# Attention scores as three fp32r products instead of one fp32 product, with the order of layer 0's blocks made anew

## The chip, the cores and the metric

The kernel runs on one core of a Trainium2 chip. The metric is the device time of one execution in microseconds; the table below gives the median of three runs and the time of the one execution that was profiled.

## The reference, cut to what matters

A decoder of two layers over 256 tokens of width 1024, all in float32. The change touches the attention of layer 0 ("stick-breaking" attention, 16 heads of 64 columns). In its core:

```python
qkv = (h @ w_qkv).reshape(b, s, 3, SB_HEADS, HEAD_DIM)
q, k, v = qkv[:, :, 0], qkv[:, :, 1], qkv[:, :, 2]
...
z = jnp.einsum('bqhd,bshd->bhqs', q_blk, k).astype(jnp.float32) * scale
causal = key_pos[None, :] < t[:, None]
log_1m = jnp.where(causal, jax.nn.log_sigmoid(-z), 0.0)
excl = lax.cumsum(log_1m, axis=3, reverse=True) - log_1m
a = jnp.where(causal, jnp.exp(jax.nn.log_sigmoid(z) + excl), 0.0)
return jnp.einsum('bhqs,bshd->bqhd', a.astype(v.dtype), v)
```

After that come the output projection, a squared-ReLU MLP, the second layer (native sparse attention and another MLP) and a last norm. None of these is edited.

## The kernel before, in words

Tokens are two tiles of 128 (T = 2). Weights arrive in pieces of 1 MB on the queue of SyncE. Each is split into a high part of type float32r (`wh`, a copy by ScalarE at line 135) and a low part, the remainder (`wl`, a subtraction by VectorE at line 138), in two halves of 1024 columns. Large products then use float32r operands: high times high, high times low and low times high. The helper `wide` (line 199) does this for products with a split activation: one matmul of 512 columns takes the high weights against both parts of the activation, one of 256 columns takes the low weights against the high part. `W` (line 143) and `step` (line 150) bring the splits in, up to two weights ahead of the one in use.

Layer 0 works on pairs of heads, eight in all, each pair filling 128 partitions. For each pair, `proj` (line 487) forms the transposed queries and keys: for each of two halves (queries, then keys), 8 matmuls of 512 columns (`qk<-xa,wh`) and 8 of 256 (`qk<-xa,wl`), 32 in all. ScalarE copies the second part out of PSUM (line 504), VectorE adds the first (line 505), and the sum is scaled with the norm's factor (line 506), on GpSimd for queries and on VectorE for keys. The result, `qkT`, is float32.

Three kinds of block follow for each pair p:

- S, `scores(p)` (line 509): four float32 matmuls of the two heads, each head in its own half of the array's rows (64 of 128), into one PSUM bank per head: 256 columns for the second tile of tokens, 128 for the first. Then the softmax-like chain: minimum with a cap on VectorE (line 525), Exp and Ln on ScalarE (529, 530), a scan (531) and a subtraction (532) on VectorE, Exp on ScalarE (533). A small memset on GpSimd (522) comes first.
- T, `turn(p)` (line 536): six transposes on TensorE of the full array, evicted by ScalarE (line 545).
- V, `values(p)` (line 548): four float32 matmuls of 64 columns of the array each (half of it per head), evicted as high and low parts (271, 272).

What stands where is written out in the table `INS` (line 38). An entry (m, k, f, p) calls block f of pair p ahead of product k of projection m; m = 8 is the output projection, where k counts slots of six matmuls each. The program's order of instructions is only a wish: a scheduler puts an instruction that is not ready by its own reckoning behind others on its engine. `high_priority` moves an eviction ahead. Once the schedule is made, each engine runs its instructions in that order.

Of the kernel before, what the change touches and what calls it, by code (L numbers as in the profile page):

```python
# [7 lines left out]
F32 = mybir.dt.float32  # L8
F32R = mybir.dt.float32r
# [5 lines left out]
P = 128  # L15
D = 1024
T = 2
NK = D // P
NH = 16
DH = 64  # L20
# [15 lines left out]
ROW = 3 * SEG  # L36

INS = (
# [4 lines left out]
)  # L43

NSA = (
# [17 lines left out]
def hybrid_kernel(ctx, tc, x, xca, xcb, eye, gcols, gfin, wqk, wva, wvb, wo0, wkv, wq, wg, rot, wo1, w1, w2, cw1, cw2, cpos, gate_b, cmask, consts, out):  # L63
    nc = tc.nc
# [8 lines left out]
    def f32(a):  # L73
        return a.bitcast(F32)
# [8 lines left out]
    def bank(name, dt=F32):  # L83
        return ps.tile([P, 512], dt, tag="a", name=name, bufs=4)

    def bank2(name):
        return ps.tile([P, 512], F32, tag="z", name=name, bufs=4)
# [55 lines left out]
    def W(i, n=None, keep=None):  # L143

        while at[0] < i or at[0] == i and n is not None and at[1] < n or at[0] == i and n is None:
            split()
        cur[0] = max(cur[0], i if keep is None else keep)
        return made[i]

    def step(k=1, end=None, pin=False):  # L150
        for _ in range(k):
            if at[0] < min(cur[0] + 3, end or len(stream)):
                split(pin)
# [30 lines left out]
    def pe(ins):  # L184
        if strict[0]:
            tc.keep_in_program_order(ins)
# [6 lines left out]
    def mm(o, a, b, first, last):  # L193
        pe(nc.tensor.matmul(o, a, b, start=first, stop=last, skip_group_check=True))  # L194
# [4 lines left out]
    def wide(o, a, xt, k, part, first, last):  # L199


        if part == 0:
            mm(o, a[0], xt[2][:, k, :, :], first, False)
        else:
            mm(o[:, 0:T * P], a[1], xt[0][:, k, :], False, last)
# [7 lines left out]
    def cut(hl, a, b):  # L213
        return hl[0][:, a:b], hl[1][:, a:b]
# [178 lines left out]
    def layer0(ap):  # L393
# [93 lines left out]
        def proj(p, hooks={}):  # L487

            w = W(i_qk[p])
            qkT = ap.tile([P, 2, T * P], F32, name="qkT", bufs=3)  # L490
            for half in range(2):
                qk = bank("qk") if p else bank2("qk")
                for j in range(2 * NK):
                    if j == 0:
                        step()
                    for f in hooks.get(2 * NK * half + j, ()):
                        f()
                    i, k = divmod(j, NK)
                    o = half * D + k * P
                    wide(qk, cut(w, o, o + P), xt, k, i, k == 0, k == NK - 1)  # L500
                lo = ap.tile([P, T * P], F32, name="qlo", bufs=2)
                o = qkT[:, half, :]
                with tc.high_priority(offset=300):
                    nc.scalar.copy(lo, qk[:, T * P:2 * T * P])
                    nc.vector.tensor_add(o, qk[:, 0:T * P], lo)
                    (nc.vector if half else nc.gpsimd).tensor_tensor(o, o, rbq[:, half], op=OP.mult)
            live[p] = qkT

        def scores(p):


            qkT = live[p]
            qT, kT = qkT[:, 0, :], qkT[:, 1, :]
            z = [bank2(f"z{hd}") for hd in range(2)]
            for hd in range(2):
                r = slice(hd * DH, (hd + 1) * DH)
                mm(z[hd][:, 0:256], qT[r, P:2 * P], kT[r, :], True, False)
            for hd in range(2):
                r = slice(hd * DH, (hd + 1) * DH)
                mm(z[hd][:, 256:384], qT[r, 0:P], kT[r, 0:P], False, True)  # L520
            e = ap.tile([P, 2 * ROW], F32, name="sbe", bufs=3)
            nc.gpsimd.memset(e.rearrange("p (b c) -> p b c", b=6)[:, :, P:SEG], NEG)
            cap = cst[:, C_CAP:C_CAP + 3 * P].rearrange("p (b c) -> p b c", b=3)
            for hd in range(2):
                nc.vector.tensor_tensor(
                    e[:, hd * ROW:(hd + 1) * ROW].rearrange("p (b c) -> p b c", b=3)[:, :, 0:P],
                    z[hd][:, 0:384].rearrange("p (b c) -> p b c", b=3), cap, op=OP.min)
            s = ap.tile([P, 2 * ROW], F32, name="sbs", bufs=2)
            nc.scalar.activation(s, e, AF.Exp)
            nc.scalar.activation(s, s, AF.Ln, bias=1.0)  # L530
            nc.vector.tensor_tensor_scan(s[:, ::-1], s[:, ::-1], go_on[:, ::-1], 0.0, OP.add, OP.mult)
            nc.vector.tensor_sub(e, e, s)
            nc.scalar.activation(e, e, AF.Exp)
            live[p] = e
# [24 lines left out]


        do = {"S": scores, "T": turn, "V": values}

        def inside(n):
# [6 lines left out]
        for n in range(NP):  # L570
            proj(n, inside(n))
# [537 lines left out]
```

## Time and profile before

| | |
|---|---|
| median of 3 runs | 616.9 us (616.69 to 617.33) |
| profiled execution | 618.14 us, of which the span of instructions is 616.4 us |
| TensorE busy | 605.6 us, 98% of the span |
| VectorE busy | 423.2 us, 69% |
| ScalarE busy | 342.2 us, 56% |
| GpSimd busy | 60.0 us, 10% |
| layer 0's projections | 28.5 to 86.75 us of the span |

The profile shows one execution. PE stands for TensorE's matmuls, PEld for its weight loads, DVE for VectorE, ACT for ScalarE, POOL for GpSimd. A row of the timeline gives start, length, engine, line, operation, output and inputs, the part of the array in use (rows * columns), the operand's shape and how many instructions were merged. Ends of matmuls are modelled, so the length of a row on PE holds some time after the next one has begun; the distance between starts is the better measure. L194 is a helper that issues most matmuls, so blocks are told apart by the names of their tiles: `qk` for the projections, `z` for S, `pa` for T, `po` for V, `acc` for the output projection.

### The profile page before, as it was taken

The page shows a single profiled execution, that of the slowest core. Times are in us where ns is not written, and L with a number is a line of the kernel's source. Part 1 is how long each engine was busy: PE and PEld are TensorE (multiplying, and loading weights), DVE is VectorE, ACT ScalarE, POOL GpSimd, SP SyncE. Part 2 cuts the span into 40 slices and gives each one's busy share as a digit, 9 for nine tenths or more (in the row PEclk, how much of TensorE's full clock was granted, in tenths as well). Part 3 has the DMA queues.
Part 4 walks back from the last instruction along what each step waited for, and adds up shares of the span by engine and source line. Part 5 has one row for each costly group of instructions (what it writes and reads, how often), then busy time and mean ns, then how long its engine had stood idle before and what let it go on. Part 6 is the DMA issues. An engine that isn't in the chain of part 4 may idle for free.

```text
span 616.4 us, 8955 instructions
## 1 busy us (share of the span) xinstructions
PE 605.6 (98%) x3477; PEld 507.1 (82%) x3477; DVE 423.2 (69%) x692; ACT 342.2 (56%) x598; POOL 60.0 (10%) x81
## 2 busy tenths in 40 slices
PE   9999999999999999999999989999999999999996
PEld 5888887888888888888998678677888888888885
DVE  5598996876666665666697799755766666556655
ACT  6667765674454444543762598854654444444441
POOL 0201110000000000000330255440000000000000
PEclk9999999999999999999999999999999999999999
DMA  8963331645555455554387831311474545545501
GB/s 308 356 265 137 137 137 69 233 176 211 199 198 196 158 204 200 192 203 153 116 258 284 277 133 69 105 68 61 152 267 158 203 187 205 204 156 198 193 1 68
DMA packets 18810, 109.33 MB, mean 177 GB/s; under 512 B 2512, under 2 KB 3792, under 8 KB 6736
## 3 DMA queue, kind: packets, MB, share of 16 engines
q1 hardware_dynamic: 17472, 107.06, 47.8%
q10 hardware_dynamic: 1296, 1.70, 0.8%
q8 instruction: 27, 0.44, 0.3%
q14 instruction: 15, 0.12, 0.1%
HBM read 106.66 MB, written 1.05 MB: 175 GB/s over the span
## 4 chain that ended last, share of the span: by engine, by line
PE 90%; DVE 3%; DMA 3%; issue 2%; ACT 1%; SPq 0%; POOLq 0%; POOL 0%; DVEq 0%; ACTq 0%
PE pu L194 29%; PE acc L189 12%; PE acc L190 11%; PE acc L191 11%; PE qk L194 7%; PE po L194 3%; PE z L194 2%; PE pk L191 2%; PE pk L189 2%; PE pk L190 2%; DMA wc<-in_cw 2%; PE ptp L197 2%; PE pv L190 1%; PE pv L191 1%; PE pv L189 1%
## 5 line engine op out<-in xcount | busy, mean ns | idle before, releaser
L138 DVE TENSOR_TENSOR wl<-raw,wh 128x1024 fp32r<-128x1024 f32 (+1 forms) x192 | 226.0, 1209 | 120.2 <-ACT wh L135 113.5
L135 ACT CAST wh<-raw 128x1024 fp32r<-128x1024 f32 (+1 forms) x192 | 190.6, 1031 | 106.4 <-PE acc L191 40.9
L194 PE MATMUL pu<-xn,wh 128*128 128x512 f32 x512 | 132.2, 392 | 0.0
L194 PEld LDWEIGHTS pu<-xn,wh 128*128 128x128 f32 x512 | 93.7, 188 | 18.0
L189 PE MATMUL acc<-wh,hh 128*128 128x512 f32 (+1 forms) x256 | 100.2, 391 | 0.0
L190 PE MATMUL acc<-wl,hh 128*128 128x512 f32 (+1 forms) x256 | 99.9, 390 | 0.0
L191 PE MATMUL acc<-wh,hl 128*128 128x512 f32 (+1 forms) x256 | 99.1, 389 | 0.0
L194 PE MATMUL pu<-xn,wl 128*128 128x256 f32 x512 | 76.5, 282 | 0.0
L194 PEld LDWEIGHTS pu<-xn,wl 128*128 128x128 f32 x512 | 72.1, 190 | 5.1
L191 PEld LDWEIGHTS acc<-wh,hl 128*128 128x128 f32 x256 | 48.1, 188 | 10.7 <-DVE hl L368 0.8
L189 PEld LDWEIGHTS acc<-wh,hh 128*128 128x128 f32 x256 | 48.2, 188 | 10.1 <-ACT hh L367 1.2
L190 PEld LDWEIGHTS acc<-wl,hh 128*128 128x128 f32 x256 | 48.2, 188 | 8.7
L367 ACT CAST hh<-ms 128x512 fp32r<-128x512 f32 x32 | 19.8, 620 | 63.1 <-DVE ms L363 63.1
L359 ACT COPY mr<-pu 128x256 f32<-128x256 f32 x64 | 23.6, 369 | 27.2 <-PE pu L194 27.2
L368 DVE TENSOR_TENSOR hl<-ms,hh 128x512 fp32r<-128x512 f32 x32 | 22.1, 692 | 19.2 <-ACT hh L367 19.2
L194 PE MATMUL qk<-xa,wh 128*128 128x512 f32 x128 | 32.5, 394 | 0.0
L360 DVE TENSOR_TENSOR mu<-pu,mr 128x256 f32<-128x256 f32 x64 | 26.6, 418 | 7.0 <-ACT mr L359 7.0
L887 POOL TENSOR_TENSOR pe<-pe,rs 128x512 f32<-128x512 f32 (+1 forms) x32 | 28.3, 917 | 25.5 <-DVE rs L882 13.6
L873 ACT ACTIVATE pe<-pe,nm 128x256 f32<-128x256 f32 (+1 forms) x64 | 28.2, 443 | 4.3 <-DVE nm L871 3.0
L194 PEld LDWEIGHTS qk<-xa,wh 128*128 128x128 f32 x128 | 22.9, 188 | 4.3 <-issue 0.2
L189 PE MATMUL acc<-wh,oT 128*128 128x512 f32 x64 | 26.3, 411 | 0.0
L191 PE MATMUL acc<-wh,oT 128*128 128x512 f32 x64 | 25.1, 392 | 0.0
(195 smaller groups left out, 828.4 us busy)
## 6 DMA issues: line engine op xcount, KB each, us to landing
raw<-in_w SPq DMA_DIRECT2D x64, 1024.0 KB, 4.8
raw<-in_wqk SPq DMA_DIRECT2D x8, 1024.0 KB, 5.1
raw<-in_wo SPq DMA_DIRECT2D x8, 1024.0 KB, 4.8
raw<-in_wkv SPq DMA_DIRECT2D x6, 1024.0 KB, 4.9
raw<-in_wq SPq DMA_DIRECT2D x4, 1024.0 KB, 6.7
wc<-in_cw SPq DMA_DIRECT2D x4, 1024.0 KB, 9.9
raw<-in_wvb SPq DMA_DIRECT2D x5, 512.0 KB, 7.1
raw<-in_wva SPq DMA_DIRECT2D x6, 256.0 KB, 5.3
```

The lines of the kernel that those rows point to most:

```text
L135: ins = nc.scalar.copy(h[:, r], raws[j][:, r])
L138: nc.vector.tensor_sub(lo[:, r], raws[j][:, r], f32(h[:, r]))
L189: pe(nc.tensor.matmul(o, a[0], b[0], start=first, stop=False, skip_group_check=True))
L190: pe(nc.tensor.matmul(o, a[0], b[1], start=False, stop=False, skip_group_check=True))
L191: pe(nc.tensor.matmul(o, a[1], b[0], start=False, stop=last, skip_group_check=True))
L194: pe(nc.tensor.matmul(o, a, b, start=first, stop=last, skip_group_check=True))
L359: nc.scalar.copy(r[:, q], pu[:, 256:512])
L360: nc.vector.tensor_add(u[:, q], pu[:, 0:256], r[:, q])
L367: nc.scalar.copy(hh, sv)
L368: nc.vector.tensor_sub(hl, sv, f32(hh))
L873: nc.scalar.activation(e, e, AF.Exp, scale=-1.0, bias=nm[:, hd, t, b:b + 1], accum_out=rs[:, hd, t, b:b + 1])
L887: nc.gpsimd.tensor_tensor(sv, sv, rs[:, hd, t, :][:, :, None].to_broadcast([P, 2, n]), op=OP.mult)
```

## The change

The scaled queries and keys are kept as two float32r parts, a high one copied by ScalarE and a low one subtracted by GpSimd, for each of the 16 halves. The scores become three products: high times high, high times low, low times high, for each head and each tile of tokens: twelve matmuls for a pair, the two heads in turn. The table `INS` is written anew.

```diff
 INS = (
-    (1, 0, 'S', 0), (3, 8, 'T', 0), (3, 24, 'S', 1), (3, 24, 'S', 2), (3, 24, 'V', 0), (4, 28, 'T', 1),
-    (5, 12, 'T', 2), (5, 16, 'V', 1), (5, 24, 'S', 3), (5, 24, 'S', 4), (5, 24, 'V', 2), (6, 29, 'T', 3),
-    (7, 12, 'T', 4), (7, 24, 'V', 3), (7, 24, 'V', 4), (7, 24, 'S', 5), (7, 24, 'S', 6), (8, 3, 'S', 7),
-    (8, 5, 'T', 5), (8, 6, 'T', 6), (8, 8, 'V', 5), (8, 8, 'V', 6), (8, 10, 'T', 7), (8, 11, 'V', 7),
+    (1, 6, 'S', 0), (3, 16, 'T', 0), (3, 18, 'S', 1), (3, 22, 'V', 0), (3, 29, 'S', 2), (4, 23, 'T', 1),
+    (5, 3, 'V', 1), (5, 16, 'T', 2), (5, 17, 'S', 3), (5, 19, 'V', 2), (5, 25, 'S', 4), (6, 24, 'T', 3),
+    (7, 17, 'T', 4), (7, 21, 'S', 5), (8, 0, 'V', 3), (8, 0, 'V', 4), (8, 0, 'S', 6), (8, 6, 'S', 7), (8, 6, 'T', 5),
+    (8, 7, 'T', 6), (8, 8, 'V', 5), (8, 8, 'V', 6), (8, 9, 'T', 7), (8, 10, 'V', 7),
 )
...
-            qkT = ap.tile([P, 2, T * P], F32, name="qkT", bufs=3)
+            qkT = ap.tile([P, 2, 2, T * P], F32R, name="qkT", bufs=3)
...
                 lo = ap.tile([P, T * P], F32, name="qlo", bufs=2)
-                o = qkT[:, half, :]
+                o = ap.tile([P, T * P], F32, name="qsum", bufs=2)
+                h, l = qkT[:, half, 0], qkT[:, half, 1]
                 with tc.high_priority(offset=300):
                     nc.scalar.copy(lo, qk[:, T * P:2 * T * P])
                     nc.vector.tensor_add(o, qk[:, 0:T * P], lo)
                     (nc.vector if half else nc.gpsimd).tensor_tensor(o, o, rbq[:, half], op=OP.mult)
+                    nc.scalar.copy(h, o)
+                    nc.gpsimd.tensor_sub(l, o, f32(h))
...
-            qT, kT = qkT[:, 0, :], qkT[:, 1, :]
             z = [bank2(f"z{hd}") for hd in range(2)]
-            for hd in range(2):
-                r = slice(hd * DH, (hd + 1) * DH)
-                mm(z[hd][:, 0:256], qT[r, P:2 * P], kT[r, :], True, False)
-            for hd in range(2):
-                r = slice(hd * DH, (hd + 1) * DH)
-                mm(z[hd][:, 256:384], qT[r, 0:P], kT[r, 0:P], False, True)
+            for t in (1, 0):
+                o, n = (256, P) if t == 0 else (0, 2 * P)
+                for i, (a, b) in enumerate(((0, 0), (0, 1), (1, 0))):
+                    for hd in range(2):
+                        r = slice(hd * DH, (hd + 1) * DH)
+                        mm(z[hd][:, o:o + n], qkT[r, 0, a, t * P:(t + 1) * P], qkT[r, 1, b, 0:n],
+                           t == 1 and i == 0, t == 0 and i == 2)
```

## The prediction

> **What bounds the kernel now.** I read the page first: span, busy shares, clock and the chain of work that ended last.
>
> ```profile
> span 616.4 us, 8955 instructions
> PE 605.6 (98%) x3477; PEld 507.1 (82%) x3477; DVE 423.2 (69%) x692; ACT 342.2 (56%) x598; POOL 60.0 (10%) x81
> PEclk9999999999999999999999999999999999999999
> PE 90%; DVE 3%; DMA 3%; issue 2%; ACT 1%; SPq 0%; POOLq 0%; POOL 0%; DVEq 0%; ACTq 0%
> ```
>
> The span is PE's: 98% busy, at full clock throughout, and 90% of the last chain. The change lies in layer 0 from the first projection (28.5 us) to the output projection, so next I took the busy times of that stretch.
>
> ```profile
> 28.50:86.75 58.25, 58.25 (x385) 49.39 (x384) 51.80 (x71) 43.27 (x69) 8.55 (x13) 1.00 0.48 176
> 86.75:112.00 25.25, 25.09 (x137) 19.67 (x136) 18.82 (x23) 15.95 (x25) 0.00 (x0) 1.00 0.25 92
> ```
>
> After stretch and length stand PE, PEld, DVE, ACT and POOL. PE has no hole in the first stretch, DVE is 89% busy (51.80 of 58.25), ACT 74%, POOL 15%. So here a microsecond of PE time is a microsecond of span, and DVE is next in line. The timeline of PE then gives what each block costs. First S (scores) of pair 0, which stands alone among the projection's products:
>
> ```profile
> 34.18 2.00 PE L194 MATMUL qk<-xa,wh 128*128 128x512 f32 x8
> 36.02 1.12 PE L194 MATMUL qk<-xa,wl 128*128 128x256 f32 x8
> 36.97 0.86 PE L194 MATMUL qk<-xa,wh 128*128 128x512 f32 x3
> 37.76 0.92 PE L194 MATMUL z<-qkT 64*128 64x256 f32 x8
> 38.61 1.42 PE L194 MATMUL qk<-xa,wh 128*128 128x512 f32 x5
> 39.87 1.11 PE L194 MATMUL qk<-xa,wl 128*128 128x256 f32 x8
> ```
>
> Starts are what counts, since ends overlap. Eight wide products take 36.02 - 34.18 = 1.84 us (0.230 each), eight narrow ones 36.97 - 36.02 = 0.95 us (0.119 each). From 36.97 to 39.87 lie 2.90 us with eight wide products in them, so S alone costs 2.90 - 1.84 = 1.06 us. Now two S and one V (values) in one run, and two V and two S:
>
> ```profile
> 49.86 2.00 PE L194 MATMUL qk<-xa,wh 128*128 128x512 f32 x8
> 51.79 1.58 PE L194 MATMUL z<-qkT 64*128 64x256 f32 x16
> 53.30 0.87 PE L194 MATMUL po<-sbt,v 128*64 128x256 f32 x8
> 54.10 1.22 PE L194 MATMUL qk<-xa,wl 128*128 128x256 f32 x8
> 55.16 2.00 PE L194 MATMUL qk<-xa,wh 128*128 128x512 f32 x8
> ...
> 80.80 2.00 PE L194 MATMUL qk<-xa,wh 128*128 128x512 f32 x8
> 82.74 1.52 PE L194 MATMUL po<-sbt,v 128*64 128x256 f32 x16
> 84.19 1.58 PE L194 MATMUL z<-qkT 64*128 64x256 f32 x16
> 85.69 1.22 PE L194 MATMUL qk<-xa,wl 128*128 128x256 f32 x8
> 86.75 0.40 PE L189 MATMUL acc<-wh,oT 128*128 128x512 f32 x1
> ```
>
> The first S takes 38.61 - 37.76 = 0.85 to the next block, two take 53.30 - 51.79 = 1.51, so a further S is 0.66 us of pure work. One V takes 54.10 - 53.30 = 0.80, two 84.19 - 82.74 = 1.45: a further V is 0.65. S alone cost 1.06, so going into the half-array form and back costs 0.40, 0.20 for each change of form. Three changes in S S V: 55.16 - 49.86 = 5.30, less 1.84 and 0.95, is 2.51, of which 1.97 is work: 0.18 each. Three in V V S S: 5.95 - 2.79 = 3.16, of which 2.62 is work: 0.18. I take 0.19. A switch between forms is a visible price that joined blocks share. T (transposes) has no such price:
>
> ```profile
> 46.41 2.01 PE L194 MATMUL qk<-xa,wh 128*128 128x512 f32 x8
> 48.26 0.82 PE L543 MATMUL pa<-ident,sbe 128*128 128x128 f32 x6
> 48.83 1.19 PE L194 MATMUL qk<-xa,wl 128*128 128x256 f32 x8
> ```
>
> It starts 1.85 us after eight wide products began, without a gap, and delays the next by 1.03 - 0.95 = 0.08; 0.65 in all.
>
> The Trainium skill, TensorEngine Tiling (Array Packing), Key Properties, says that changing the tiling mode drains TensorE; the trace agrees, with 0.18 to 0.20 us a change, and by that rule it would hold for fp32r as well, against this change: the 1.5 us below stand with it and go without it.
>
> **The change, part by part.**
>
> *The products.* Before, a pair's scores are four fp32 products, recorded as eight matmuls, two each. After, they are twelve fp32r products: for each head three of 256 columns and three of 128. The two heads run beside each other in the two row halves: 16 records in 1.51 us before, though taken one by one at the paces of full fp32r products (0.119 for 256 columns, 0.111 for 128, below) they would need 8 x 0.119 + 8 x 0.111 = 1.84. So I count a head pair as one.
>
> ```profile
> 608.97 0.27 PE L190 MATMUL accq<-wl,hh 128*128 128x128 f32 x1
> ...
> 610.09 0.28 PE L191 MATMUL accq<-wh,hl 128*128 128x128 f32 x1
> ```
>
> These are fp32r products of 128 columns, ten steps in 1.12 us: 0.111 each, hardly under the 0.119 of 256 columns, because the weight load before each is as long for both. S becomes 3 x 0.119 + 3 x 0.111 = 0.69 us instead of 0.66: **+0.03 x 8 = +0.25 us**. The 256-column half gains, and the 128-column half, where the load sets the pace, loses it again. No trace shows fp32r in row halves. Bounds: if pace followed columns (0.119 and 0.06), S would be 0.54 and the eight a gain of 1.0 us; if heads took turns, 6 x 0.119 + 6 x 0.111 = 1.38 and a loss of 5.8 us. I take 0.69, from the nearest rows.
>
> *The places.* I count changes of form along both tables. Before: S0; S1 S2 V0; V1; S3 S4 V2; V3 V4 S5 S6; S7; V5 V6; V7, which is 2+3+2+3+3+2+2+2 = 19. After: S0 to S5 and V0 to V2 each stand alone (18), then V3 V4 S6 (3), S7, V5 V6 and V7 (2 each): 27. T is a full-array transpose and needs no change. **8 x 0.19 = +1.5 us.**
>
> *The one stall that goes.*
>
> ```profile
> 90.63 0.39 PE L191 MATMUL acc<-wh,oT 128*128 128x512 f32 x1
> 91.18 0.92 PE L194 MATMUL z<-qkT 64*128 64x256 f32 x8 [0.16 <-DVE qkT L506]
> ```
>
> The next start was due at 90.63 + 0.23, and with the half a change (0.1) at 90.96: S7 waits 0.2 us for its keys. At slot 6 of the output projection instead of 3 it comes some 4 us later: **-0.2 us**.
>
> *The splits on ACT and POOL.* Each of 16 halves gets a copy (ACT) and a subtraction (POOL).
>
> ```profile
> L504 ACT COPY qlo<-qk x16: 350/373/414, 31.6 to 88.2; 128x256 f32<-128x256 f32 x16
> L506 POOL TENSOR_TENSOR qkT<-qkT,rbq x8: 733/740/1655, 32.5 to 84.3; 128x256 f32<-128x256 f32 x8
> L138 DVE TENSOR_TENSOR wl<-raw,wh x26: 1200/1218/1778, 26.9 to 111.5; 128x1024 fp32r<-128x1024 f32 x26
> ```
>
> ACT: 16 x 0.37 = 6 us more in a stretch where it idles for 58.25 - 43.27 = 15 us. POOL: 16 x 0.74 = 12 us more, with 50 us idle; at its worst 16 x 1.65 = 26, which still fits. Neither is the bound by itself; what counts is the longer way to S, and DVE.
>
> The way: the copy waits on ACT's queue for the multiplication by the norm, which for queries is POOL's, and behind it wait the weights' casts, the exponentials and T's evictions; behind the subtraction on POOL wait the next multiplication and S's small memset. In the trace the slowest way from a half's last product to its scaled keys is that of pair 6:
>
> ```profile
> 77.38 0.84 PE L194 MATMUL qk<-xa,wh 128*128 128x512 f32 x3
> 83.44 0.41 DVE L506 TENSOR_TENSOR qkT<-qkT,rbq 128x256 f32<-128x256 f32 x1
> ```
>
> From the projection's end (77.38) to 83.85 are 6.5 us; copy and subtraction add 1.1 to 2.0, so 7.6 to 8.5. In the new table S6 comes after all of projection 7 (5.58), T4 (0.65), S5 (0.69 + 0.38) and V3 V4 with two changes (1.30 + 0.38): 9.0 us after its own projection's end. The same walk gives 8.7 us for S4, 8.2 for S2 and more for the others, whose ways were shorter: margins of 0.2 us or more, so no stall is counted. T7 is tighter:
>
> ```profile
> 95.50 1.02 DVE L525 TENSOR_TENSOR sbe<-z,cst 128x384 f32<-128x384 f32 x2
> 101.25 0.85 ACT L533 ACTIVATE sbe<-sbe 128x774 f32<-128x774 f32 x1 [1.40 <-DVE sbe L532]
> ```
>
> Pair 7's softmax took 95.50 to 102.10, 6.6 us, with little beside it. In the new table T7 starts 8.0 us after S7: S7 and the change back (0.88), T5 and T6 (1.30), three slots of six products (3 x 1.37), V5 V6 with two changes (1.68). Less 0.8 for S itself 7.2 are left, and T5, T6, V5 and V6 want ACT and DVE in that time. Bounds 0 and 1.5 us (four evictions of 0.37 in the way), taken as **+0.2 us**, near zero since no T waited before.
>
> DVE: the maximum of L138, 1.78 against a median of 1.22, falls beside a POOL product that took 1.40 instead of 0.74, so the two hold each other up, by 0.6 us at most. Sixteen more meetings cost DVE nothing at best and 16 x 0.56 = 9 us at worst, against 6.5 us idle here and 6.4 in the next stretch. The weights are split up to two tiles ahead of PE (line 152), so this is hidden as a rule; without cover it is the third rival.
>
> The Trainium skill, SBUF — State Buffer, "SBUF: two separate sides", says that a DVE instruction with two SBUF inputs and a GpSimd instruction exclude each other for the whole instruction. The trace agrees in part: one side of a meeting gained 0.6 us. By the rule alone DVE's worst would be 16 x 0.74 = 12 us instead of 9, which is still the third rival's case.
>
> **Sum:** 1.5 + 0.25 - 0.2 + 0.2 = +1.75 us. The profiled execution took 618.14 us (span 616.4 and 1.74 around it), so it becomes 619.9; the median before, 616.9, lies 1.2 below that execution, and I forecast 616.9 + 1.7 = **618.6 us**.
>
> **The rivals.**
>
> *Load-free pace, 617.4 or less.* If 128-column pairs in row halves go by columns, S gains 1.0 us in all: 1.5 - 1.0 - 0.2 + 0.2 = +0.5. Against it: the accq rows. Chance 0.10.
>
> *The price of a switch belongs to fp32 and not to the half array: faster.* Then the 16 changes into and out of S cost nothing, and only the 11 of V remain: 11 x 0.19 = 2.1 against 19 x 0.19 = 3.6, -1.5, with +0.25 and -0.2: 615.4. It decides if entry and exit of S fall under 0.1 us each. For it: S and its neighbours differ in type as well as in form. Against it: V's changes cost the same, and T, fp32 on the full array, joins without a gap. Chance 0.15.
>
> *The longer way decides.* POOL and DVE meet, S2, S4, S6 and T7 each wait some 0.7 us: +2.8 on top, 621.4. For it: DVE at 89%, ways of 6.5 us. Against it: the margins. Chance 0.14.
>
> *Heads take turns in fp32r:* 5.8 instead of 0.25, so 624.2. Against it: they overlap in fp32. Chance 0.06.
>
> *The places aren't kept.* S0 stands at slot 0 of projection 1 and ran 19 products later, since what isn't ready is put behind. If blocks join again, the 1.5 goes: about 617.1. Chance 0.05.
>
> **Chances and range.** The forecast keeps 0.50, of which 0.11 end under the bound of 0.2% (1.2 us, about what a measurement here can tell). Faster: 0.13 of the switch rival. Same: 0.11 + 0.02 + 0.10 + 0.05 = 0.28. Slower: 0.39 + 0.14 + 0.06 = 0.59. The range reaches from the switch rival (615.4) to near the longer way (621.2) and leaves out the heads in turn and the tail of the waits. The forecast's own range is 617.6 to 619.6.
>
> **What would show it.** S in twelve records, a lone S at 1.05 to 1.15 us between its neighbours; single runs of S and V at 27 changes; no wait before S7; POOL some 20 us busy by 87 us; the first product of the MLP about 1.7 us later than before, and everything behind it moved by as much. I am wrong if a lone S costs under 0.8 us (switch or pace), over 1.6 (turns), or if PE waits by name for POOL, ACT or DVE at S or T for over 1 us in all.

## The result and the profile after

The changed kernel takes 625.5 us (median of four runs, 625.11 to 625.71) against 616.9 us before (four runs, 616.69 to 617.33): a ratio of 1.0146, with a 95% interval of 1.0134 to 1.0158. It is slower, as forecast, but by 8.6 us where 1.7 were forecast, and it lies above the range. The profiled execution took 625.11 us, of which the span is 623.3 us. First its page: the span, the busy shares, the granted clock in 40 slices of the span, and the shares of the chain that ended last.

```profile
span 623.3 us, 9047 instructions
PE 609.0 (98%) x3509; PEld 509.4 (82%) x3509; DVE 426.9 (68%) x692; ACT 346.6 (56%) x614; POOL 78.5 (13%) x97
PEclk9999899999999999999999999999999999999998
PE 84%; DVE 6%; ACT 3%; issue 3%; POOL 2%; DMA 2%; POOLq 0%; DVEq 0%
```

PE is busy only 3.4 us longer, while the span grew by 6.9: half of the growth is idle time of PE. The fifth slice and the last have a clock below 9, which no slice of before had (the last lies far behind all that was edited), and the chain has lost 6 points of PE, most of them to DVE, ACT and POOL.

Layer 0 can be cut out exactly. It begins with the first projection product (`qk`) and ends where the MLP's first product (`pu`) starts: 28.50 to 115.58 us before, 27.38 to 123.19 after. Here is each kernel's row of that stretch (length, then busy time of PE, PEld, DVE, ACT and POOL with the number of instructions, granted clock, share and rate of the DMA engines). Before:

```profile
28.50:115.58 87.08, 86.92 (x540) 72.03 (x539) 74.19 (x97) 61.08 (x96) 8.55 (x13) 1.00 0.42 152
```

After:

```profile
27.38:123.19 95.81, 91.05 (x572) 74.20 (x570) 78.27 (x98) 66.16 (x113) 27.65 (x29) 0.98 0.39 142
```

The stretch is 8.73 us longer, about the difference of the medians. The two profiled spans differ by only 6.9, because the changed kernel reached its first projection 1.1 us sooner and was 0.7 us faster behind layer 0, where nothing was edited. Length less PE's busy time is PE's idle time: 0.16 us before, 4.76 after. The waits of PE in it have names (engine, tile, line, the releaser, then us in total, times, longest):

```profile
PE pa L546 <- ACT sbe L536: 2.5, 2, 1.3
PE po L194 <- ACT sbt L548: 2.1, 1, 2.1
PE z L194 <- POOL qkT L509: 0.2, 1, 0.2
```

So T (`pa`) waits twice for the chain's last Exp, V (`po`) once for the copies of T's transposes out of PSUM, and S hardly at all. The timeline of PE shows the longest wait, before V1:

```profile
61.04 0.82 PE L546 MATMUL pa<-ident,sbe 128*128 128x128 f32 x6
...
65.80 1.27 PE L194 MATMUL po<-sbt,v 128*64 128x256 f32 x8 [2.06 <-ACT sbt L548]
66.99 2.50 PE L194 MATMUL qk<-xa,wh 128*128 128x512 f32 x5
69.29 1.57 PE L194 MATMUL qk<-xa,wl 128*128 128x256 f32 x8
```

T1's transposes were through before 62 us. Three engines' timelines show why their copies came out so late. ACT:

```profile
64.96 0.41 ACT L508 CAST qkT<-qsum 128x256 fp32r<-128x256 f32 x1 [2.12 <-POOL qsum L507]
65.27 0.85 ACT L548 COPY sbt<-pa 128x384 f32<-128x384 f32 x2
```

POOL and DVE at that time:

```profile
62.81 2.12 POOL L507 TENSOR_TENSOR qsum<-qsum,rbq 128x256 f32<-128x256 f32 x1 [8.02 <-DVE qsum L506]
```

```profile
62.65 1.76 DVE L534 TENSOR_TENSOR_SCAN sbs<-sbs,go_on 128x774 f32<-128x774 f32 x1
64.44 1.31 DVE L535 TENSOR_TENSOR sbe<-sbe,sbs 128x774 f32<-128x774 f32 x1
```

The queries' product on POOL starts beside DVE's scan and takes 2.12 us where the shortest of these takes 0.73. The new copy of the high part stands at the head of ACT's queue for it and idles 2.12 us; the transposes' copies, which need nothing that is late, are queued behind it; V1 is behind those. ACT's waits from 28 to 95 us hold this six times, 10.5 us in all; with two smaller rows the copies stand for 13.6 us:

```profile
ACT qkT L508 <- POOL qsum L507: 10.5, 6, 2.3
ACT qkT L508 <- DVE qsum L507: 1.9, 3, 0.9
ACT qkT L508 <- POOL sbe L525: 1.2, 1, 1.2
```

The Trainium skill, SBUF — State Buffer, "SBUF: two separate sides", says that a GpSimd instruction and a DVE instruction with two SBUF inputs lock each other out for a whole instruction. These rows agree in the main: the product starts 0.16 us after the scan, ends 0.52 us after the scan's end, and takes 1.4 us longer than the shortest. The prediction had counted 0.6 us for such a meeting, from VectorE's side; its own row of POOL's products has a maximum of 1.66 us, 0.9 over the median.

After that wait the clock fell. The five wide products behind V1 (66.99 to 69.29) took 2.30 us, where five take 1.15 at the 0.230 us of before. The windows row of the 4.4 us from 66.0 on:

```profile
66.00:70.40 4.40, 4.40 (x19) 3.46 (x18) 3.26 (x5) 3.60 (x7) 1.79 (x4) 0.61 0.07 24
```

At a granted clock of 0.61 the stretch does the work of 4.40 x 0.61 = 2.68 us, so another 1.7 us are lost without any wait being shown. The budget of the 8.7 us is then 4.6 us of idle time, 1.7 of clock, and 2.4 of longer work. The first experiment finds 1.7 of these 2.4 in the table's eight more changes of form. Two changes more were not in the table: in this profile S0 runs in two pieces, at 37.33 and, behind one projection product, at 38.37. At the same price they are some 0.4 us, an estimate.

### The profile page after: what moved, and what is told of

Same layout as the page of the kernel before. It is cut to its first block, busy times and chain, and to the rows that moved or that the text cites. A ratio compares the mean times of both kernels' runs of the same rounds, so it can differ in the third digit from the quotient of the medians.

```text
span 623.3 us, 9047 instructions
## 1 busy us (share of the span) xinstructions
PE 609.0 (98%) x3509; PEld 509.4 (82%) x3509; DVE 426.9 (68%) x692; ACT 346.6 (56%) x614; POOL 78.5 (13%) x97
## 3 DMA queue, kind: packets, MB, share of 16 engines
HBM read 106.66 MB, written 1.05 MB: 173 GB/s over the span
## 4 chain that ended last, share of the span: by engine, by line
PE 84%; DVE 6%; ACT 3%; issue 3%; POOL 2%; DMA 2%; POOLq 0%; DVEq 0%
PE pu L194 29%; PE acc L189 12%; PE acc L191 11%; PE acc L190 11%; PE po L194 3%; PE pk L191 2%; PE pk L189 2%; PE pk L190 2%; DVE wl L138 2%; PE z L194 2%; DMA wc<-in_cw 2%; PE qk L194 2%; PE ptp L197 1%; POOL qsum L507 1%; PE pv L189 1%
## 5 line engine op out<-in xcount | busy, mean ns | idle before, releaser
L189 PEld LDWEIGHTS acc<-wh,hh 128*128 128x128 f32 x256 | 48.2, 188 | 10.1 <-ACT hh L367 1.2
L194 PE MATMUL qk<-xa,wh 128*128 128x512 f32 x128 | 36.1, 412 | 0.0
L759 POOL TENSOR_TENSOR fold<-ident 128x60 f32<-128x60 f32 x1 | 1.3, 1265 | 205.0 <-PE acc L191 205.0
## 6 DMA issues: line engine op xcount, KB each, us to landing
wc<-in_cw SPq DMA_DIRECT2D x4, 1024.0 KB, 10.1
```

The lines of the kernel that those rows point to most:

```text
L189: pe(nc.tensor.matmul(o, a[0], b[0], start=first, stop=False, skip_group_check=True))
```

## The experiments

**Theories before the runs.** The *queue theory*: the new copy ties ACT's queue to POOL's product, and with it everything queued there. Its rivals: the *table theory* (the new places put T and V too close behind S), the *product theory* (fp32r products in half rows are dear) and the *load theory* (16 copies are simply too much for ACT). The expectations name three more: *meetings* (POOL's subtractions hold up VectorE's chain), *way* (the scores come later because their operands pass two more steps) and *slack* (the split makes the softmax's way longer and the new places leave no room for it). The edits are against the changed kernel, or the kernel before where that is said. One table for all runs first. The ratio is to runs of the kernel before taken beside each group (medians 615.9 to 616.9 us). All columns behind it come from the one profiled execution of each kernel, whose time can lie up to 1.3 us off the median. "Longer" is layer 0's stretch, qk to pu, less the 87.08 us of before; "idle" is the stretch less PE's busy time; "spells" counts the waits that were followed by a granted clock of 0.61 to 0.66 over 4.4 us behind them, each put at 1.7 us; "rest" is what remains of "longer" (the 0.16 us of idle time before taken out).

| kernel | median, us | ratio to before [95%] | longer | idle | spells | rest |
|---|---|---|---|---|---|---|
| the change | 625.5 | 1.0146 [1.0134, 1.0158] | 8.7 | 4.8 | 1 | 2.4 |
| e1 new table, fp32 | 618.6 | 1.0038 [1.0023, 1.0053] | 1.7 | 0.1 | 0 | 1.7 |
| e2 old table, fp32r | 635.3 | 1.0307 [1.0292, 1.0322] | 18.4 | 10.8 | 4 | 0.9 |
| e3 queries' product on DVE | 623.0 | 1.0110 [1.0095, 1.0125] | 5.9 | 3.2 | 0 | 2.9 |
| e4 subtractions on DVE | 630.6 | 1.0231 [1.0214, 1.0248] | 14.0 | 7.3 | 3 | 1.8 |
| e5 fp32r products, no splits | 617.9 | 1.0034 [1.0018, 1.0050] | 1.6 | 0.3 | 0 | 1.5 |
| e6 splits, fp32 products | 622.8 | 1.0107 [1.0092, 1.0122] | 6.2 | 3.8 | 0 | 2.6 |
| e7 copy by the multiplying engine | 622.6 | 1.0101 [1.0084, 1.0118] | 7.3 | 3.8 | 1 | 2.0 |
| e8 the same, a copy on ACT beside it | 622.7 | 1.0115 [1.0090, 1.0139] | 5.7 | 2.9 | 0 | 3.0 |
| e9 later T and V | 630.1 | 1.0213 [1.0189, 1.0237] | 12.7 | 5.8 | 2 | 3.6 |
| e10 joined blocks, fp32r | 631.9 | 1.0257 [1.0241, 1.0273] | 14.3 | 9.0 | 1 | 3.8 |
| e11 joined blocks, fp32 | 621.1 | 1.0079 [1.0063, 1.0095] | 4.5 | 3.6 | 0 | 1.1 |
| e12 V1's wait filled | 625.7 | 1.0150 [1.0128, 1.0171] | 7.3 | 2.7 | 0 | 4.7 |
| e13 copy from ready data | 621.7 | 1.0086 [1.0069, 1.0102] | 4.6 | 2.1 | 0 | 2.7 |
| e14 copy, no subtraction | 623.6 | 1.0116 [1.0101, 1.0131] | 7.8 | 4.2 | 1 | 2.0 |
| e15 e7 with T4 later, S0 later | 625.2 | 1.0146 [1.0122, 1.0170] | 8.0 | 3.8 | 1 | 2.7 |

**e1, the new table alone.** The kernel before with the changed kernel's `INS`:

```diff
-    (1, 0, 'S', 0), (3, 8, 'T', 0), (3, 24, 'S', 1), (3, 24, 'S', 2), (3, 24, 'V', 0), ...
+    (1, 6, 'S', 0), (3, 16, 'T', 0), (3, 18, 'S', 1), (3, 22, 'V', 0), (3, 29, 'S', 2), ...
```

> Only the new table, products in fp32 as before, no copy and no subtraction. Queue theory (ACT stands at the copy of the high part of the queries until POOL has multiplied, and T's evictions and the last Exp stand behind it): none of that is here, so only the eight more changes of form and the vanished wait of S7 are left, +1.0 to +1.6 us, 618.2 us; PE waits for nothing at T0, V1 and T4. Table theory (the new places leave T and V too little time): PE waits at T0, V1 and T4 as in the changed kernel, 622 to 625 us.

618.6 us, and in its stretch of layer 0 PE waits for no one by name:

```profile
27.77:116.52 88.75, 88.62 (x540) 72.04 (x539) 74.83 (x97) 61.05 (x96) 9.93 (x13) 1.00 0.42 150
```

PE's busy time is 1.70 us longer than before for the same 540 instructions: with 8 more changes of form, 0.21 us each. (By the medians the kernel is 2.3 us longer, 1.4 to 3.3.) The prediction's largest term holds (0.19 each, 1.5). The table theory falls: by itself the table makes no PE wait.

**e2, the old table with the splits.** The changed kernel with the `INS` of before.

> The split and the fp32r products, with the table of before. Queue theory: ACT still stands some 10 us at the copy behind POOL's products, so PE still waits for T or V or S for 3 to 8 us, without the 1.5 us of the changes of form: 620 to 625 us. Table theory: as before plus 0.25 us, 617.2 us.

635.3 us, far more than either theory gave. The waits of PE in its stretch:

```profile
PE pa L546 <- ACT sbe L536: 7.6, 3, 2.8
PE z L194 <- ACT qkT L508: 2.4, 1, 2.4
PE z L194 <- POOL qkT L509: 0.8, 2, 0.5
```

10.8 us of waits, and four spells of low clock, 4 x 1.7 = 6.8: together 17.6 of the 18.4 us. The splits need the room of the new table; that table costs 1.7 us and saves 10 against the old one.

**e3, the queries' product on DVE; e4, the subtractions on DVE.** If it is POOL being slow beside DVE that ACT stands for, the product on DVE should end it.

```diff
-                    (nc.vector if half else nc.gpsimd).tensor_tensor(o, o, rbq[:, half], op=OP.mult)
+                    nc.vector.tensor_tensor(o, o, rbq[:, half], op=OP.mult)
```

> The changed kernel with the multiplication of the queries on VectorE instead of GpSimd (8 x 0.41 us more for VectorE); the subtractions stay on GpSimd. Queue theory: ACT's copy no longer waits for POOL, its waits fall from 10.5 us to under 4, PE's waits at T0, V1 and T4 and the slow clock after V1 go: 618.2 to 619.5 us. Load theory (the 6 us of copies on ACT are too many): nothing gained, 624 to 626 us. Meetings theory (POOL's sixteen subtractions hold up VectorE's chain): half is left, 622 us or more.

```diff
-                    nc.gpsimd.tensor_sub(l, o, f32(h))
+                    nc.vector.tensor_sub(l, o, f32(h))
```

> The changed kernel with the sixteen subtractions on VectorE instead of GpSimd (16 x 0.41 us more for VectorE); the multiplication of the queries stays on GpSimd. Queue theory: ACT still waits for POOL's product wherever that meets a scan of VectorE; 622 to 626 us. Meetings theory: POOL has only 8 products left, as before the change, so the waits go: 618 to 620 us.

e3 gained 2.5 us of 8.6 and missed its forecast. ACT's waits in 28 to 95 us show why:

```profile
ACT qkT L508 <- DVE qsum L507: 9.9, 12, 1.7
```

10 us of the 13.6 of standing are left, now for DVE. So the theory was too narrow: the copy stands for whichever engine multiplies, and that engine has work of its own ahead (DVE is busy 79.8 of the 93.0 us of e3's stretch). e4 put more onto DVE and lost 5 us: T waited 4.6 us, V 2.7, with three spells of low clock. That is not the 618 to 620 us of the meetings theory, but the edit also loads DVE, so it does not test that theory alone; e13 and e14 do.

**e5 and e6, the products alone and the splits alone.** e5 has the multiplication write float32r at once, and all three products read that one part, so the low parts are left out; e6 keeps the four fp32 products and makes high and low parts that nothing reads.

```diff
-                    (nc.vector if half else nc.gpsimd).tensor_tensor(o, o, rbq[:, half], op=OP.mult)
-                    nc.scalar.copy(h, o)
-                    nc.gpsimd.tensor_sub(l, o, f32(h))
+                    (nc.vector if half else nc.gpsimd).tensor_tensor(h, o, rbq[:, half], op=OP.mult)
...
-                        mm(z[hd][:, o:o + n], qkT[r, 0, a, t * P:(t + 1) * P], qkT[r, 1, b, 0:n],
+                        mm(z[hd][:, o:o + n], qkT[r, 0, t * P:(t + 1) * P], qkT[r, 1, 0:n],
```

> New table and twelve fp32r products, but no split: the multiplication writes one rounded part, and all three products read it (the low parts are left out, so the scores are not the reference's). If the products cost what fp32r on the full array does, 0.25 us more than the new table alone (618.6 us): 618.3 to 619.4 us. If heads hinder each other or PE's queue runs dry with twelve short products, 620 to 625 us.

```diff
-                o = ap.tile([P, T * P], F32, name="qsum", bufs=2)
-                h, l = qkT[:, half, 0], qkT[:, half, 1]
+                o = qkT[:, half, :]
+                h, l = hl[:, half, 0], hl[:, half, 1]
...
```

> New table and the four fp32 products of before, with ACT's copy and POOL's subtraction made beside them and read by nothing. Queue theory, after the third run in this form: it is the copy on ACT that stands and waits for the product, whoever makes the product, and what stands behind it on ACT comes late; so nearly all of the loss is here, 623 to 626 us, and PE waits for T or V, not for S. Way theory (the scores themselves come later because their operands pass two more steps): 618.6 to 620 us, since the scores don't read the split.

This pair settles which half of the change costs. With twelve fp32r products and no splits the stretch is 1.64 us longer than before, the same as e1's 1.67 with four fp32 ones: the products cost nothing beyond the table. With the splits and the fp32 products it is 6.2 us longer. The product theory is out, and the way theory with it for the larger part, since in e6 the scores read nothing of the split and T still waits 3.6 us. The 2.5 us between e6 and the change are, in the main, V1's wait and its spell of low clock (2.1 and 1.7 us), less the 1.1 us that T waits longer in e6; behind e6's longest wait, 1.97 us at T2, the clock stayed at 1.00.

**e7 and e8, the copy on the engine that multiplies.** Then nothing of it stands in ACT's queue. e8 adds 16 copies of the same size on ACT from data that is ready, to test load by itself.

```diff
-                    nc.scalar.copy(h, o)
+                    (nc.vector if half else nc.gpsimd).tensor_copy(h, o)
```

> The changed kernel, with the copy of the high part made by the engine that multiplied (GpSimd for queries, VectorE for keys), so ACT never stands behind a product. Queue theory: ACT's waits for qsum are none, PE's waits at T0, V1 and T4 fall under 1 us in all: 618.8 to 620.5 us. Way theory or meetings theory (GpSimd has 8 more operations, VectorE 8 more): 623 us or more.

e8 is e7 with

```diff
+                    dm = ap.tile([P, T * P], F32R, name="dm", bufs=2)
+                    nc.scalar.copy(dm, lo)
```

> As the run before, with a copy of the same size on ACT in each half that reads what ACT itself has just written and that nothing reads (6 us more of ACT, no waiting). Queue theory: at most 1 us over the run before. Load theory: the loss comes back, 623 to 626 us.

Both came to 622.6 or so. The load theory is out: 16 more copies on ACT add nothing to the median. But e7 missed its forecast. ACT no longer stands for a product, and the waits came back in other places: S0 waits for POOL's subtraction of the keys, which starts when DVE's copy is done and takes 1.64 us where the shortest takes 0.73; T4 waits for an Exp that waits 2.4 us for DVE, whose scan starts 9.3 us after S4's start, 7.3 in e1. PE in its stretch:

```profile
PE pa L546 <- ACT sbe L536: 2.4, 2, 2.2
PE z L194 <- POOL qkT L509: 1.2, 1, 1.2
```

**e9, e10 and e11, other places.** e9 puts T and V of pairs 0 to 4 and 7 later, which gave T 11 us or more after its S (9.5 for pair 7); e10 joins blocks (V1 V2 S3 S4 and so on) to save changes of form; e11 is e10's table in the kernel before.

```diff
-    (1, 6, 'S', 0), (3, 16, 'T', 0), (3, 18, 'S', 1), (3, 22, 'V', 0), (3, 29, 'S', 2), (4, 23, 'T', 1),
+    (1, 6, 'S', 0), (3, 18, 'S', 1), (3, 26, 'T', 0), (3, 29, 'S', 2), (4, 6, 'V', 0), (4, 28, 'T', 1),
...
```

> The changed kernel, with T and V of pairs 0 to 4 and 7 put later in the table (T0 at slot 26 of projection 3, T2 at the end of projection 5, T4 at slot 30 of projection 7, each V behind its T), S where it was. Slack theory: copy and subtraction make the softmax's way 1 to 3 us longer on whichever engine they lie, and the new table has no slack for it at T0, T2, T4 and V1; with 11 us or more from each S to its T nothing of it reaches PE, PE waits under 1 us in all, though ACT still waits for POOL: 618.2 to 619.8 us. Rival (copy and subtraction hold PE up wherever the blocks stand, by S or by the weights): 621 us or more.

```diff
-    (1, 6, 'S', 0), (3, 16, 'T', 0), (3, 18, 'S', 1), (3, 22, 'V', 0), (3, 29, 'S', 2), (4, 23, 'T', 1),
+    (1, 6, 'S', 0), (3, 20, 'T', 0), (3, 31, 'V', 0), (3, 31, 'S', 1), (3, 31, 'S', 2), (5, 6, 'T', 1),
...
```

> The changed kernel with a table that joins blocks (S1 S2 with V0, S3 S4 with V1 V2, S5 S6 with V3 V4: 17 changes of form instead of 27) and leaves 8 to 12 us from S to T. Slack theory with the price of a change of form: 616.9 + 0.25 - 0.4 = 616.7 if no T or V waits, up to 618.5 if those at 8 us do. Rival (the split costs as such): 621 us or more.

> The kernel before with the same joined table: two changes of form fewer, and S7 a slot later. By the price of a change of form 0.4 us less, and 0.2 for the wait of S7: 616.3 us, within what can be measured of before. If what is joined or moved matters in another way, it is 0.5 us or more off.

All three missed, e9 and e10 by far. In e9 T waits hardly any more, but the waits have moved:

```profile
PE acc L189 <- DVE oT L272: 2.7, 1, 2.7
PE po L194 <- ACT sbt L548: 2.4, 1, 2.4
PE pa L546 <- ACT sbe L536: 0.3, 1, 0.3
```

Pair 2's way from S to its last Exp was 16.7 us in e9, against 12.7 in the changed kernel. Moving a block of PE also moves what its chain meets on ACT and DVE, so a margin read off one table does not carry over to the next. e11 shows the same without any split: joined blocks should have been cheaper than before, and cost 4.5 us more, 3.5 of them in waits before T and V. The rest in e9 and e10, 3.6 and 3.8 us, is above that of every other kernel but e12. In e9, 31 changes of form, four more than in e1, are some 0.8 us of it; the remainder is not explained.

**e12, V1's wait filled.** Ten products of zeros ahead of V1, into a bank that nobody reads, so that PE doesn't idle.

```diff
+            if p == 1:
+                wm = bank2("warm")
+                for _ in range(10):
+                    mm(wm, zero[:, 0:P], zero, True, True)
```

> The changed kernel with ten products of zeros (512 columns, 2.2 us, read by nothing) ahead of V1, in the 2 us in which PE waits there. If the half clock of the 4 us behind V1 comes from that wait, the clock stays up and 1.5 to 2.1 us are gained: 623.4 to 624 us. If the clock drops for another reason, 625.5 us or up to 2.2 more.

The windows row of the same stretch as above:

```profile
66.00:70.40 4.40, 4.40 (x28) 3.13 (x27) 3.01 (x5) 4.29 (x8) 2.12 (x3) 1.00 0.30 121
```

The clock stays at 1.00, and layer 0 is 1.5 us shorter than in the changed kernel, close to the 1.7 of the spell (the ten products, 2.3 us at 0.23 each, stand in this kernel's rest and take the place of V1's wait of 2.06): idle time of PE was the cause of the low clock. The median does not show a gain (625.7 us, runs from 623.85 to 626.64): the profiled execution, the longest of the four, lost 1.1 us ahead of layer 0 and 1.9 behind it against the change's, where nothing was edited. So as a gain in time it stays unproved.

**e13 and e14, standing and subtraction apart.** In e13 the copy reads data that is ready, so that it never stands, and the subtraction stays (the high part is then not that of the scaled sum). In e14 the copy stands and the subtraction is left out; all three products read the high part.

```diff
-                    nc.scalar.copy(h, o)
+                    nc.scalar.copy(h, lo)
```

> The changed kernel, but ACT's copy reads what ACT has just copied out of PSUM instead of the scaled sum, so it has its size and its place and never stands behind a product; GpSimd subtracts as before (the high parts are then not the scaled sum's, so the scores are not the reference's). Standing theory (ACT stands behind the product, and T's evictions and the last Exp stand behind ACT): V1's wait and the half clock after it go, T0's too; at most T4's is left, 619 to 621.5 us. Meetings theory (GpSimd's subtractions and VectorE hold each other up, and the softmax's way grows): most of the loss stays, 622.5 us or more.

```diff
-                    nc.gpsimd.tensor_sub(l, o, f32(h))
...
-                        mm(z[hd][:, o:o + n], qkT[r, 0, a, t * P:(t + 1) * P], qkT[r, 1, b, 0:n],
+                        mm(z[hd][:, o:o + n], qkT[r, 0, 0, t * P:(t + 1) * P], qkT[r, 1, 0, 0:n],
```

> The changed kernel with ACT's copy, which stands behind the product, and without GpSimd's subtraction; all three products read the high part (the low parts are left out, so the scores are not the reference's). Standing theory: most of the loss stays, 621.5 us or more, with ACT waiting some 10 us for the product. Meetings theory: as with neither of the two (617.9 us), 618 to 619.5 us.

The waits of PE in e13:

```profile
PE pa L546 <- ACT sbe L536: 1.3, 1, 1.3
PE z L194 <- POOL qkT L509: 0.8, 1, 0.8
```

and in e14:

```profile
PE pa L545 <- ACT sbe L535: 2.3, 2, 1.3
PE po L194 <- ACT sbt L547: 1.9, 1, 1.9
```

With e5 (neither) and the change (both) this makes a square. Layer 0 is longer than before by 1.64 us with neither, 4.56 with the subtractions alone, 7.75 with the standing copy alone, 8.73 with both. So the standing copy is the larger part: 6.1 us alone, 4.2 on top of the subtractions. The subtractions make 2.9 alone and 1.0 on top. By the medians (differences of the ratios, times 616.5 us) the copy's part is smaller, 5.1 alone and 3.7 on top, and the subtractions' 3.2 and 1.9, but the order is the same. Of these four kernels V1's wait and the spell of low clock are in the two whose copy stands; in e3 and e6 the copies also stand (9.9 and 7.6 us) without that spell. e13's 621.7 us lies just above the standing theory's range and below that of the meetings theory: the subtractions do cost something by themselves. Where e13's T4 waits, the reason is DVE and not ACT. The scan of pair 4 starts 7.9 us after S4's start, 7.3 in e1, and takes 2.27 us instead of 1.76 beside POOL's product, so the last Exp waits for DVE.

**e15, room where e7 waited.** e7 with T4 behind S5 and S0 14 products later:

```diff
-    (1, 6, 'S', 0), ... (7, 17, 'T', 4), (7, 21, 'S', 5),
+    (1, 20, 'S', 0), ... (7, 21, 'S', 5), (7, 22, 'T', 4),
```

> The run with the copies made by the multiplying engine (622.5 us), with T4 at slot 22 of projection 7 behind S5 instead of slot 17 ahead of it, and S0 at slot 20 of projection 1; nothing else moved. That run's profile has waits of 2.3 us at T4 and 1.6 us at S0. If these are a lack of slack at two places, both go: 618.7 to 620 us. If the wait moves along with the block, 621.5 us or more.

```profile
PE z L194 <- POOL qkT L509: 1.8, 2, 1.2
PE acc L189 <- DVE qsum L506: 1.7, 1, 1.7
PE pa L546 <- ACT sbe L536: 0.2, 1, 0.2
```

e7's rows show waits of 2.2 us at T4 and 1.2 at S0, not the 2.3 and 1.6 of the expectation. T4's went, S0's stayed, and the output projection, which in e7 waited for nothing, now waits 1.7 us for a sum on DVE: 625.2 us, no better than the change. None of the versions beats the kernel before.

## Why the prediction was wrong in size, step by step

*The products: right.* A block S between projection products in the changed kernel, and a lone one among narrow products:

```profile
51.33 0.91 PE L194 MATMUL z<-qkT 64*128 64x256 f32 x12
52.16 1.19 PE L194 MATMUL qk<-xa,wh 128*128 128x512 f32 x4
...
54.66 0.76 PE L194 MATMUL qk<-xa,wl 128*128 128x256 f32 x5
55.35 0.90 PE L194 MATMUL z<-qkT 64*128 64x256 f32 x12
56.18 0.62 PE L194 MATMUL qk<-xa,wl 128*128 128x256 f32 x3
56.64 1.99 PE L194 MATMUL qk<-xa,wh 128*128 128x512 f32 x8
```

S runs in twelve records and takes 52.16 - 51.33 = 0.83 us to the next block, 0.85 before. The lone one costs 56.64 - 54.66 - 0.95 = 1.03 us; 1.05 to 1.15 had been named, from 1.07. The heads run beside each other in fp32r, so that rival is out, and e5 against e1 puts the eight pairs at no difference (1.64 and 1.67 us) where +0.25 was taken.

*The places: right in kind and nearly in size.* +1.5 was said for 27 changes of form, and e1, with 27, measures +1.7. The changed kernel had 29, since S0 ran in two pieces. The rival by which the price belongs to fp32 is out as well: e5 has fp32r products in the same table and pays the same.

*The wait of S7: right.* No wait before S7 is left.

*The splits: wrong, and this is the step that failed.* The text gave ACT 6 us more and found that of the two "Neither is the bound by itself"; for the ways to S it said "margins of 0.2 us or more, so no stall is counted", and for T it took 0.2 us, "near zero since no T waited before". The busy times came out much as said: ACT 4.4 us more (342.2 to 346.6), POOL 18.5 (60.0 to 78.5, between the 12 taken and the 26 at worst), DVE 3.7 (423.2 to 426.9), and no wait of PE for weights in layer 0. The margins of S held: only S0 waited, 0.2 us. T7, the one T that was checked, did not wait either. The stalls came at T0, V1 and T4, which were not checked. The way that T needs runs from S's start to the end of the last Exp, and the text took it from pair 7, whose chain has "little beside it": 6.6 us. Pair 4's was in the same profile, in the timelines of PE and ACT before:

```profile
67.77 1.58 PE L194 MATMUL z<-qkT 64*128 64x256 f32 x16
78.14 0.86 ACT L533 ACTIVATE sbe<-sbe 128x774 f32<-128x774 f32 x1 [1.12 <-DVE sbe L532]
```

S4 is the second half of that run and begins at about 68.5; the Exp ends at 79.00: 10.5 us, not 6.6. The new table gives it little more. In e1, with nothing split:

```profile
69.87 0.92 PE L194 MATMUL z<-qkT 64*128 64x256 f32 x8
81.21 0.88 PE L543 MATMUL pa<-ident,sbe 128*128 128x128 f32 x6
80.31 0.85 ACT L533 ACTIVATE sbe<-sbe 128x774 f32<-128x774 f32 x1 [1.73 <-DVE sbe L532]
```

The Exp ends at 81.16 and T4 starts at 81.21: 0.05 us to spare, on a way of 11.3 us. In the changed kernel S4 starts at 75.46. Then, on DVE and on ACT:

```profile
84.26 1.32 DVE L535 TENSOR_TENSOR sbe<-sbe,sbs 128x774 f32<-128x774 f32 x1
84.79 0.41 ACT L508 CAST qkT<-qsum 128x256 fp32r<-128x256 f32 x1 [2.14 <-POOL qsum L507]
85.11 1.05 ACT L135 CAST wh<-raw 128x1024 fp32r<-128x1024 f32 x1
86.06 0.84 ACT L548 COPY sbt<-pa 128x384 f32<-128x384 f32 x2
86.80 0.38 ACT L505 COPY qlo<-qk 128x256 f32<-128x256 f32 x1
87.06 0.87 ACT L536 ACTIVATE sbe<-sbe 128x774 f32<-128x774 f32 x1
```

and on PE:

```profile
87.98 0.88 PE L546 MATMUL pa<-ident,sbe 128*128 128x128 f32 x6 [1.32 <-ACT sbe L536]
```

What the Exp reads is ready at 85.58, 10.1 us after S4's start and no later than in e1 (10.4). But the copy stands 2.14 us for POOL, what had queued behind it runs first, and the Exp starts 1.5 us late and ends at 87.93, 12.5 us after S4's start. T4 waits 1.32 us. T0 goes the same way: what its Exp reads is ready at 47.95, a copy stands 2.32 us until 48.58, and the Exp starts at 49.15. The text had named these very things ("behind it wait the weights' casts, the exponentials and T's evictions") and priced them at nothing: it took idle time of ACT on average for room in ACT's queue. Each engine here runs its instructions in the order of the schedule, so an instruction that waits costs its wait (up to 2.3 us here), not its 0.37 us, to all that is behind it.

*What was not in the sum at all* is the clock: 1.7 us that follow from a wait of 2 us.

*The rival "the longer way decides"* (2.8 us more, at S2, S4, S6 and T7) had part of the mechanism, the meetings of POOL and DVE, but at the wrong places (S0, T0, V1 and T4 waited), without the queue on ACT, and at less than half the size (6.3 us with the clock). The sign of failure that the text named, PE waiting by name "at S or T for over 1 us in all", came up: 2.7 us there, and 2.1 at V.

*Still open:* how the subtractions' part (2.9 us alone) divides between POOL and DVE holding each other up and the changed order of ACT's and DVE's work, since the edits can also change that order (at e13's T4 0.5 us is the longer scan and 0.6 its later start); and why e9 and e10 lost as much as they did. A kernel with the order of ACT and DVE held fixed wasn't tried.

## What to carry to other kernels

Before a short instruction is added to an engine with spare time, look at what it will wait for and at what stands behind it on that engine: the price is the wait, paid by the work behind, and moving the instruction to another engine tends to move the wait along. Take the length of a chain from the busiest place where the profile shows it, and check every consumer of it against the new places, not only the one that looks tight. With TensorE 98% busy, one wait near 2 us is paid almost twice, by itself and by the clock after it.

## What the runs showed of the hardware

A wait of TensorE near 2 us mostly slows what comes behind it. Over all kernels, 15 named waits in layer 0 were 1.89 us or longer (up to 2.84), and 13 of them were followed by a mean granted clock of 0.61 to 0.66 over 4.4 us (the two others, 1.97 and 2.32 us, by 1.00). Of 17 waits from 0.9 to 1.8 us only one (1.68 us) was. The Trainium skill, TensorE: Matmul & The Clock Gate, "Why this matters for your kernels", advises against idle gaps above some 3 us between bursts. Here shorter waits were enough, and the measurement decides; a sharp limit does not show.

POOL's product of 128x256 took 0.73 us at the shortest and 2.12 us beside a DVE scan with two SBUF inputs, and DVE's subtraction behind the scan took 1.31 us instead of 0.96. Twelve fp32r products in the two row halves took no longer than four fp32 ones (0.83 us and 0.85 us to the next block). One after the other, at the full array's paces of 0.119 and 0.111 us, they would need 1.38 us, by estimate, so the two heads overlap.
